# First norm of a two-layer hybrid backbone: modulation weights in four units of two feature tiles, k and the first q tile summed unit by unit

## The chip, the cores and the metric

The kernel runs on one core of one Trainium2 chip. A core has TensorE (matmuls into PSUM; the profile splits it into PE, the matmuls, and PEld, the weight loads), VectorE (DVE), ScalarE (ACT), GpSimd (POOL) and SyncE (SP, which here only issues DMAs). The metric is the device time of one execution in microseconds (us). Before the change it is 1147.22 us, the median of 3 runs (1147.14 to 1147.23).

## The reference, cut to what matters

Two layers work on 256 latent tokens (x) and 256 context tokens (ctx) of 1024 features. The part that the change touches is the very first step of layer 0: an RMS norm of both streams, its modulation by two vectors that are themselves matrix products, and the first columns of the input projection.

```python
m_lat = jnp.split((silu(c)     @ mod_w[0] + mod_b[0]), 6)      # shift, scale, gate, ...
m_ctx = jnp.split((silu(c_ctx) @ mod_w[0] + mod_b[0]), 6)
h_lat = rms_norm(x,   norm_g[0, 0]) * (1 + m_lat[1]) + m_lat[0]
h_ctx = rms_norm(ctx, norm_g[0, 0]) * (1 + m_ctx[1]) + m_ctx[0]
p  = h_lat @ even_w_in          # q, k, v of the attention, inputs of the HGRN2 heads
pc = h_ctx @ even_w_in
```

All of the rest (window attention, HGRN2, output projection, SwiGLU, then the retention layer with its own) follows from `p` and `pc`, and reaches the output through a long row of projections.

## The kernel before, in words

Features lie on the 128 partitions, so the 1024 features are 8 feature tiles, and a tile of `h` is 128 features by 512 tokens (256 latent, then 256 context). Every projection is done in three matmuls for each weight block of 128 by 128: the weight's rounded part times the rounded `h`, the same times the remainder of `h`, and the remainder of the weight times the rounded `h` (`mm3`, lines 336 to 338). The weights come as pieces of 8 blocks (512 KB, `load_raw`, line 258, three buffers); ACT makes the rounded part (`whi`, line 268), DVE the remainder (`wlo`, line 269), up to `LOOK` = 2 pieces ahead (`ensure`, four buffers).

The start of the kernel, in order of the program: `small`, 129 KB of constants, `x` in 8 DMAs of 128 KB, `ctx` in 4 of 256 KB, and then the modulation weights of shift and scale, 8.4 MB as 32 DMAs of 256 KB (line 130). They are four quarters of eight tiles: two for scale (chunk 1), two for shift (chunk 0), each 512 output features wide. The second half of these tiles borrows buffers of the weight pieces, of the later modulation weights (`mr`) and of `h`.

Inside a block with a manual schedule (lines 485 to 524) each engine keeps the order of the program: squares (ACT, line 445) and their sum over the feature tiles (DVE, line 449), one matmul with ones for each stream (line 453), Ln and Exp for the reciprocal root (lines 290 and 456); then for each quarter the product `mod0a` (16 matmul instructions, line 175, a copy to SBUF on ACT, line 178) and `mod0b` (4 small products that turn it onto the partitions, line 185, and `mod_finish` on DVE, lines 154 and 158). `scaled` (DVE, line 459) needs scale alone; `shifted` makes the rounded `h` (ACT, line 465) and the remainder (DVE, line 466) and needs shift, that is the last two quarters. Pieces 0 to 2 are converted among these.

Outside the manual block a planner fixes each engine's order: an instruction that is ready may be put into a gap of an engine ahead of earlier lines. The first such instructions are `p1`, the group with the columns of k and of the first q tile (line 891): all latent columns with the feature tile as the outer loop, then all context columns (2 tiles of columns, 8 feature tiles, 3 matmuls, twice, so 96 matmuls of 256 columns). Then `p2` (the other q tiles and v, 96 matmuls of 512 columns, pieces 2 to 5) and `tokgroup`. Each 1600 columns of such work call `tick`, which lets background work proceed: the later modulation vectors (`mod_one`, one task of 512 KB for each `MODE` = 2.3 ticks in this stage, two for a task that runs on TensorE) and the lanes of the attention.

Of the kernel before, what the change touches and what calls it, by code (L numbers as in the profile page):

```python
# [7 lines left out]
F32 = mybir.dt.float32  # L8
# [3 lines left out]
AF = mybir.ActivationFunctionType  # L12
ALU = mybir.AluOpType
# [19 lines left out]
N_PIECE = N_BLOCKS // PIECE  # L33
LOOK = 2
# [3 lines left out]
FA = 2  # L38
PES = [3]
ORD = [2, 3, 4, 5]  # L40
MODE = 2.3
TICK = 1600
ADEL = 5
HD1,HD2,HD3,HD4=[1, 1, 1, 2]
# [18 lines left out]
S_LB = S_OG + 1  # L63
# [5 lines left out]
def hybrid_kernel(ctx, tc, xT, wst, mw0, mwT, small, cbc, cst, imask, dmat, out, order):  # L69
    nc = tc.nc  # L70
# [34 lines left out]
    x = [cp.tile([P, L], F32, tag=f"x{k}", name=f"x{k}") for k in range(KD)]  # L105
    xc = [u((P, 2, L)) for _ in range(KD // 2)]
    for k in range(KD):
        nc.sync.dma_start(x[k][:], xT[:, k, LAT])
    for k in range(KD // 2):
        nc.sync.dma_start(xc[k][:], xT[:, 2 * k:2 * k + 2, CTX])  # L110

    def xs(k, s):
        return x[k][:] if s == 0 else xc[k // 2][:, k % 2, :]

    con0 = [u() for _ in range(3)]
    mws = []
    for i in range(32):
        if 16 <= i < 22:
            if i % 2 == 0:
                pair = rawp.tile([P, 2, NT], F32, tag="raw", name=nm("raw"))  # L120
            t = pair[:, i % 2, :]
        elif 22 <= i < 28:
            if i % 2 == 0:
                pair = mp.tile([P, D], F32, tag="mr", name=nm("mr"))
            t = pair[:, (i % 2) * NT:(i % 2 + 1) * NT]
        elif i < 16:
            t = u()[:]
        else:
            t = hp.tile([P, NT], F32, tag="h", name=nm("mw"))[:]
        nc.sync.dma_start(t, mw0[i // 8, i % 8])  # L130
        mws.append(t)
# [123 lines left out]
    def load_raw(r):  # L255
        if r not in raws:
            t = rawp.tile([P, RAW, P], F32, tag="raw", name=nm("raw"))
            nc.sync.dma_start(t[:].rearrange("p b n -> p (b n)"), wst[r])
            raws[r] = t

    def ensure(p):
        for q in range(len(pieces), min(p + LOOK, N_PIECE - 1) + 1):
            r = q
            load_raw(r)
            src = raws.pop(r)
# [153 lines left out]
    class Norm:  # L419
# [6 lines left out]
        def pre(self, k):  # L426

            hi, lo = u(dt=F32R), u(dt=F32R)
            sh = mvec(self.l, self.s, 3 * self.j, k).to_broadcast([P, 2])
            split(sh, hi[:, L:LW], lo[:, L:LW])  # L430
            g = gsv[:, self.l, self.j, self.s, k:k + 1]
            A.activation(hi[:, LAT], x[k][:], AF.Copy, scale=g)
            V.scalar_tensor_tensor(lo[:, LAT], x[k][:], g, hi[:, LAT].bitcast(F32), ALU.mult, ALU.subtract)
# [47 lines left out]
    def upd(l, ch, s, m, ps):  # L481
        sl = LAT if s == 0 else CTX
        V.scalar_tensor_tensor(xs(m, s), ps[:, sl], mvec(l, s, ch, m), xs(m, s), ALU.mult, ALU.add)  # L483

    manual[0] = True
    with tc.manual_schedule():
        h = new_h()
        ns = [Norm(0, 0, s, h) for s in range(2)]
        for n in ns:
            for k in range(KD):  # L490
                n.add(k)
            n.stats()
        for r in range(3):
            load_raw(r)
        ts_ = [u() for _ in range(KD)]

        def scaled(s, ks):
            for k in ks:
                ns[s].scaled(k, ts_[k][:, ns[s].sl])

        mod0a(0)
        mod0a(1)
        mod0b(0)
        scaled(0, range(4))
        mod0a(2)
        mod0b(1)
        scaled(0, range(4, 8))
        scaled(1, range(4))
        mod0a(3)
        mod0b(2)  # L510
        scaled(1, range(4, 8))
        mod0b(3)
# [5 lines left out]
        for n in ns:
            for k in range(KD):
                if n.s == 0 and k in (1, 4):  # L520
                    ensure(k // 4 - LOOK)
                n.shifted(k, ts_[k][:, n.sl])
        ensure(0)
# [9 lines left out]
    omh = cp.tile([P, 4], F32, tag="omh", name="omh")
    nomh = cp.tile([P, 4], F32, tag="nomh", name="nomh")
    lbh = cp.tile([P, 4], F32, tag="lbh", name="lbh")
    l0, l1 = sml[:, S_LB:S_LB + 4], sml[:, S_LB + 4:S_LB + 8]
    mx, e0, e1 = sm(4), sm(4), sm(4)
    V.tensor_tensor(mx, l0, l1, ALU.max)
    V.tensor_tensor(e0, l0, mx, ALU.subtract)
    V.tensor_tensor(e1, l1, mx, ALU.subtract)  # L540
    A.activation(e0, e0, AF.Exp)
    A.activation(e1, e1, AF.Exp)
    V.tensor_tensor(e1, e0, e1, ALU.add)
    V.reciprocal(e1, e1)
    V.tensor_tensor(e0, e0, e1, ALU.mult)
    V.tensor_scalar(omh[:], e0, -0.5, 0.5, ALU.mult, ALU.add)
    V.tensor_scalar(nomh[:], e0, 0.5, -0.5, ALU.mult, ALU.add)
    V.tensor_scalar(lbh[:], e0, 0.5, 0.5, ALU.mult, ALU.add)
# [770 lines left out]
```

## Time and profile before

| | |
|---|---|
| median of 3 runs | 1147.22 us |
| the profiled execution | 1146.45 us, of which the span of the trace 1144.6 us |
| PE busy | 1116.4 us (98%) |
| PEld busy | 996.9 us (87%) |
| DVE busy | 767.4 us (67%) |
| ACT busy | 554.0 us (48%) |
| HBM read | 177.56 MB, 156 GB/s over the span |

The page gives each engine's busy time and its share of the span, and the chain of work that ended last. Idle time of an engine that is not the bottleneck costs nothing. A timeline row gives start, duration, engine, line, operation, output and inputs, the count of merged instructions, and in brackets the idle time before them with what ended it. An engine's name with a q is its queue: SPq rows are issues of DMAs and not the transfers. A matmul's duration includes its pipeline, so the rate of a series is read from the distance of the starts.

### The profile page before, as it was taken

The numbers are of one execution on the slowest core, as the hardware profiler recorded it, in microseconds if no ns is written. First come the engines' busy times: TensorE is split into PE (matmuls) and PEld (weight loads), VectorE is DVE, ScalarE is ACT, GpSimd is POOL, SyncE is SP. The second block draws the span as 40 slices with busy tenths as digits, with TensorE's granted clock in tenths as the row PEclk, the third lists the DMA queues.
The fourth block names the chain that finished last, engine by engine and source line by source line (L and its number), as shares of the span: only waits on it lengthen the run. The fifth ranks groups of instructions, "written<-read, shape, count | busy, mean of one in ns | idle before, by whom it ended". The sixth has DMA issues, their size and how long they took to land.

```text
span 1144.6 us, 18866 instructions
## 1 busy us (share of the span) xinstructions
PE 1116.4 (98%) x7514; PEld 996.9 (87%) x7514; DVE 767.4 (67%) x1399; ACT 554.0 (48%) x948; POOL 20.8 (2%) x46
## 2 busy tenths in 40 slices
PE   3999999999999999999999998999999999999998
PEld 1777877888998888988888898999999999999998
DVE  3877698899798557357883678374646577555553
ACT  5676676664753231123322476454445657544441
POOL 0012000000000000000000000000000000000000
PEclk9999999999999999999999999999999999999999
DMA  9987221326237446247983324343434265655553
GB/s 329 349 235 184 92 65 66 112 74 202 94 113 241 143 147 202 77 139 237 324 308 109 95 75 129 111 131 109 148 94 147 92 203 167 192 183 181 184 183 109
DMA packets 56121, 182.46 MB, mean 159 GB/s; under 512 B 6368, under 2 KB 9824, under 8 KB 55904
## 3 DMA queue, kind: packets, MB, share of 16 engines
q1 hardware_dynamic: 53648, 176.45, 47.6%
q0 software_dynamic: 2240, 4.72, 1.7%
q8 instruction: 59, 0.97, 0.4%
q14 instruction: 30, 0.25, 0.1%
q10 hardware_dynamic: 144, 0.08, 0.0%
HBM read 177.56 MB, written 1.05 MB: 156 GB/s over the span
## 4 chain that ended last, share of the span: by engine, by line
PE 84%; DVE 10%; ACT 3%; DMA 1%; issue 1%; DVEq 0%; ACTq 0%; SPq 0%
PE mm L338 23%; PE mm L337 23%; PE mm L336 23%; PE ax L337 2%; PE ax L336 2%; PE ax L338 2%; DVE wlo L269 2%; DMA raw<-in_wst_dram 1%; PE ax L175 1%; PE ax L656 1%; ACT whi L268 1%; PE ax L675 1%; DVE u L459 1%; PE mm L411 1%; PE mm L409 1%
## 5 line engine op out<-in xcount | busy, mean ns | idle before, releaser
L268 ACT ACTIVATE whi<-raw 128x1024 fp32r<-128x1024 f32 x230 | 243.3, 1059 | 403.0 <-PE mm L337 242.9
L269 DVE TENSOR_TENSOR wlo<-raw,whi 128x1024 fp32r<-128x1024 f32 x230 | 280.7, 1222 | 166.5 <-ACT whi L268 165.9
L336 PE MATMUL mm<-hh,whi 128*128 128x256 f32 (+1 forms) x1072 | 362.2, 339 | 1.2 <-ACT whi L268 0.9
L338 PE MATMUL mm<-hh,wlo 128*128 128x256 f32 (+1 forms) x1072 | 361.6, 338 | 0.6 <-DVE wlo L269 0.6
L337 PE MATMUL mm<-hl,whi 128*128 128x256 f32 (+1 forms) x1072 | 362.0, 338 | 0.1
L337 PE MATMUL mm<-u,whi 128*128 128x256 f32 (+2 forms) x768 | 236.9, 309 | 0.0
L338 PE MATMUL mm<-u,wlo 128*128 128x256 f32 (+2 forms) x768 | 236.7, 308 | 0.0
L336 PE MATMUL mm<-u,whi 128*128 128x256 f32 (+2 forms) x768 | 236.3, 308 | 0.3 <-DVE x L483 0.3
L338 PEld LDWEIGHTS mm<-hh,wlo 128*128 128x128 f32 x1072 | 204.4, 191 | 21.8 <-DVE wlo L269 0.8
L336 PEld LDWEIGHTS mm<-hh,whi 128*128 128x128 f32 x1072 | 204.2, 191 | 21.9 <-ACT whi L268 0.9
L337 PEld LDWEIGHTS mm<-hl,whi 128*128 128x128 f32 x1072 | 204.3, 191 | 20.2 <-DVE hl L466 0.3
L336 PEld LDWEIGHTS mm<-u,whi 128*128 128x128 f32 x768 | 146.4, 191 | 7.9 <-issue 0.4
L338 PEld LDWEIGHTS mm<-u,wlo 128*128 128x128 f32 x768 | 146.6, 191 | 7.2
L337 PEld LDWEIGHTS mm<-u,whi 128*128 128x128 f32 x768 | 146.6, 191 | 7.1
L233 DVE CUSTOM_DVE_ANT_0 mr<-mr,cb 128x1024 f32<-128x1024 f32 x72 | 87.1, 1222 | 13.2 <-DMA mr<-in_mwT_dram 12.6
L416 ACT ACTIVATE u<-u 128x512 fp32r<-128x512 f32 (+1 forms) x84 | 43.0, 526 | 36.7 <-DVE u L1007 17.3
L1007 DVE TENSOR_TENSOR u<-u,mm 128x512 f32<-128x512 f32 (+1 forms) x40 | 22.1, 553 | 44.7 <-PE mm L338 44.7
L233 DVE CUSTOM_DVE_ANT_0 u<-mr,cb 128x1024 bf16<-128x1024 f32 x40 | 48.4, 1219 | 2.8 <-DMA mr<-in_mwT_dram 1.5
L417 DVE TENSOR_TENSOR u<-u,u 128x512 fp32r<-128x512 f32 (+1 forms) x84 | 46.5, 565 | 5.0 <-ACT u L416 4.9
L336 PE MATMUL ax<-u,u 128*128 128x256 f32 x160 | 45.9, 287 | 3.1 <-ACT u L416 3.1
L483 DVE SCALAR_TENSOR_TENSOR x<-mm,modv,x 128x256 f32<-128x256 f32 x48 | 22.4, 480 | 36.1 <-PE mm L338 36.1
L337 PE MATMUL ax<-u,u 128*128 128x256 f32 x160 | 46.0, 287 | 0.0
(220 smaller groups left out, 1216.4 us busy)
## 6 DMA issues: line engine op xcount, KB each, us to landing
raw<-in_wst_dram SPq DMA_DIRECT2D x230, 512.0 KB, 3.8
mr<-in_mwT_dram SPq DMA_DIRECT2D x80, 512.0 KB, 4.5
u<-in_mw_dram SPq DMA_DIRECT2D x16, 256.0 KB, 5.2
u<-u POOLq DMA_DIRECT2D x20, 128.0 KB, 5.7
u<-in_dmat_dram POOLq DMA_DIRECT2D x8, 256.0 KB, 3.0
raw<-in_mw_dram SPq DMA_DIRECT2D x6, 256.0 KB, 5.2
mr<-in_mw_dram SPq DMA_DIRECT2D x6, 256.0 KB, 5.2
x<-in_xT_dram SPq DMA_DIRECT2D x8, 128.0 KB, 3.4
```

The costliest lines, as they stand in the source:

```text
L175: T.matmul(ps[32 * g:32 * g + 32, :], cT[:, k, :], mws[nt * 8 + k], start=(k < 4), stop=(k >= 4), skip_group_check=True)
L233: V.tensor_tensor_reduce(o, mr[:], cb[:, s, :], 1.0, 0.0, ALU.mult, ALU.add, mvec(l, s, ch, k))
L268: A.activation(hi[:], src[:], AF.Copy)
L269: V.tensor_tensor(lo[:], src[:], hi[:].bitcast(F32), ALU.subtract)
L336: T.matmul(o, w[0], a[0], start=first, stop=False, skip_group_check=shared)
L337: T.matmul(o, w[0], a[1], start=False, stop=False, skip_group_check=shared)
L338: anchor[0] = T.matmul(o, w[1], a[0], start=False, stop=last, skip_group_check=shared)
L409: T.matmul(ps[t][:], a[0], w[0], start=(k == 0), stop=False)
L416: A.activation(hi, src, AF.Copy)
L417: V.tensor_tensor(lo, src, hi.bitcast(F32), ALU.subtract)
L483: V.scalar_tensor_tensor(xs(m, s), ps[:, sl], mvec(l, s, ch, m), xs(m, s), ALU.mult, ALU.add)
L1007: V.tensor_tensor(g[:, 0:w], g[:, 0:w], ps[2 * i + 1][:, 0:w], ALU.mult)
```

## The change

The modulation weights of shift and scale are laid out in four units. Unit p holds scale and shift of feature tiles 2p and 2p+1 (256 columns of each), so one `mod0a`/`mod0b` gives all that these two tiles of `h` need. `x` is loaded in two DMAs of 512 KB with 4 KB in a row on a partition (before: 1 KB), `ctx` in four with 2 KB in a row. The order of the DMAs is: unit 0, x, ctx, weight piece 0, units 1 and 2, piece 1, and after the first feed unit 3, piece 2 and the constants. The sum of squares over feature tiles is taken on TensorE (16 products with ones in float32, no sums on DVE), squares are of two feature tiles each, Ln and Exp use one table set, loaded once with the constants of the HGRN2 gates. `mod0a` leaves its result in PSUM, and `mod0b` makes the copy.

`p1` is written into the manual block: `dense(k)` does all 512 tokens of feature tile k for both column tiles (6 matmuls of 512 columns), between the products of the units. Only pieces 0 and 1 are converted in the block (`look[0]` is 0 in it and `LOOK` after). `p1` calls no `tick`; `MODE` is 1.9 for 2.3.

```diff
-MODE = 2.3
+MODE = 1.9
...
-        parts[nt] = u()
-        A.activation(parts[nt][:], ps[:], AF.Copy)
-
-    def mod0b(nt):
-        ch, half = 1 - nt // 2, nt % 2
-        part = parts[nt]
+        parts[p] = ps
+
+    def mod0b(p):
+        part = u()
+        A.activation(part[:], parts[p][:], AF.Copy)
...
+        for i, ch in enumerate((1, 0)):
+            mod_finish(0, ch, 2 * p, 2 * p + 2, ps2[:, 2 * i:2 * i + 2, :].rearrange("p c s -> p s c"))
...
+        load_raw(0)
+        mw_load(1)
+        mw_load(2)
+        load_raw(1)
+        lb_consts()
+        mod0a(0)
+        mod0b(0)
+        stat = []
         for n in ns:
+            ps = axb()[:, 0:L]
+            for j in range(4):
+                q = u((P, 2, L))
+                src = xl[j // 2][:, 2 * (j % 2):2 * (j % 2) + 2, :] if n.s == 0 else xc[j][:]
+                if n.s and j % 2:
+                    V.tensor_tensor(q[:], src, src, ALU.mult)
+                else:
+                    A.activation(q[:], src, AF.Square)
+                for i in range(2):
+                    T.matmul(ps, ones, q[:, i, :], start=(j + i == 0), stop=(j + i == 4))
+            stat.append(ps)
+        for n, ps in zip(ns, stat):
+            n.r = u()[:, 0:L]
+            A.activation(n.r, ps, AF.Ln, bias=epst[:], scale=1.0 / D)
+            A.activation(n.r, n.r, AF.Exp, scale=-0.5)
...
+        def dense(k, js):
+            for j in js:
+                w = take('ein', k, j)
+                o = p1[j][:]
+                T.matmul(o, w[0], HS[k][0], start=(k == 0), stop=False)
+                T.matmul(o, w[0], HS[k][1], start=False, stop=False)
+                anchor[0] = T.matmul(o, w[1], HS[k][0], start=False, stop=(k == KD - 1))
+
+        def feed(p):
+            for k in (2 * p, 2 * p + 1):
+                t = scaled(k)
+                if k % 4 == 0:
+                    ensure(k // 4)
+                shifted(k, t)
+
         mod0a(1)
+        feed(0)
+        mw_load(3)
+        load_raw(2)
...
+        dense(0, J)
+        mod0b(1)
+        feed(1)
+        dense(1, J)
+        mod0a(2)
+        dense(2, J)
+        mod0b(2)
+        feed(2)
+        dense(3, J)
+        mod0a(3)
+        dense(4, J)
+        mod0b(3)
+        feed(3)
+        for k in range(5, KD):
+            dense(k, J)
         A.activation(cb[:], cb[:], AF.Silu)
...
-    p1 = group('ein', [E_AK, E_AQ], K8, HS, sls=(LAT, CTX))
```

## Rows read from the trace of the kernel before

**Rows 1.** The page: the busy line of the engines (us, share of the span, instructions), and the chain that ended last, by engine.

```profile
PE 1116.4 (98%) x7514; PEld 996.9 (87%) x7514; DVE 767.4 (67%) x1399; ACT 554.0 (48%) x948; POOL 20.8 (2%) x46
...
PE 84%; DVE 10%; ACT 3%; DMA 1%; issue 1%; DVEq 0%; ACTq 0%; SPq 0%
```

**Rows 2.** Busy time by stretch: the stretch and its length, busy us of PE, PEld, DVE, ACT, POOL (with counts), the granted clock of TensorE as a share of full, the busy share of the DMA engines, GB/s.

```profile
0.00:50.82 50.82, 31.39 (x197) 20.57 (x197) 28.00 (x73) 32.03 (x57) 1.25 (x6) 0.97 0.94 348
50.82:95.00 44.18, 44.18 (x189) 34.52 (x188) 36.36 (x64) 28.71 (x37) 5.32 (x11) 1.00 0.74 215
```

**Rows 3.** Timeline of PE from the statistics to the first sum of `p1`.

```profile
19.10 1.22 PE L453 MATMUL ax<-u,con 128*128 128x256 f32 x2 [6.54 <-DVE u L449]
20.25 5.73 PE L175 MATMUL ax<-u,cT 128*32 128x512 f32 x32
25.91 1.05 PE L185 MATMUL ax<-con,u 128*128 128x2 f32 x8
...
33.73 1.95 PE L185 MATMUL ax<-con,u 128*128 128x2 f32 x16
36.53 0.50 PE L336 MATMUL mm<-hh,whi 128*128 128x256 f32 x2 [0.85 <-ACT whi L268]
```

**Rows 4.** Timeline of PEld in the products of the quarters: four loads at the lower and at the upper rate, and the wait for the last tile of the modulation weights.

```profile
23.67 0.20 PEld L175 LDWEIGHTS ax<-u,cT 128*32 128x32 f32 x4 [0.66 <-issue]
24.52 0.12 PEld L175 LDWEIGHTS ax<-u,cT 128*32 128x32 f32 x4 [0.65 <-DMA raw<-in_mw_dram]
24.95 0.12 PEld L175 LDWEIGHTS ax<-u,cT 128*32 128x32 f32 x4 [0.31 <-issue]
...
32.75 0.14 PEld L175 LDWEIGHTS ax<-mw,cT 128*32 128x32 f32 x2 [0.51 <-DMA mw<-in_mw_dram]
```

**Rows 5.** Timeline of PE: two sums of `p1` at the lower rate, the last of `p1`, and the first two of `p2`.

```profile
40.73 0.41 PE L336 MATMUL mm<-hh,whi 128*128 128x256 f32 x1
40.95 0.41 PE L337 MATMUL mm<-hl,whi 128*128 128x256 f32 x1
...
50.70 0.28 PE L338 MATMUL mm<-hh,wlo 128*128 128x256 f32 x1
50.82 0.40 PE L336 MATMUL mm<-hh,whi 128*128 128x512 f32 x1
51.05 0.40 PE L337 MATMUL mm<-hl,whi 128*128 128x512 f32 x1
```

**Rows 6.** Busy time by stretch, columns as in rows 2, around the start of `p1`.

```profile
35.00:36.00 1.00, 0.67 (x7) 0.59 (x6) 1.00 (x3) 0.98 (x2) 0.00 (x0) 1.00 1.01 404
...
37.00:38.00 1.00, 0.53 (x3) 0.30 (x2) 1.00 (x2) 1.00 (x3) 0.00 (x0) 1.00 1.03 382
38.00:39.00 1.00, 0.78 (x3) 0.78 (x4) 1.00 (x4) 1.00 (x3) 0.00 (x0) 0.58 1.13 443
39.00:40.00 1.00, 1.00 (x7) 1.00 (x6) 1.00 (x2) 1.00 (x4) 0.00 (x0) 0.50 1.01 425
...
41.50:42.00 0.50, 0.50 (x6) 0.50 (x5) 0.50 (x3) 0.50 (x2) 0.00 (x0) 0.93 1.00 410
```

**Rows 7.** Timeline of ACT and DVE together, in order of time: the copy of a late line, the statistics' last Exp, the copy of a quarter's result, `mod_finish`, `scaled`, the conversions, `shifted`, and the Silu of `cb`.

```profile
6.74 0.29 ACT L1042 ACTIVATE idr<-con 128x128 fp32r<-128x128 f32 x1
...
20.85 1.28 ACT L456 ACT_TABLE_LOAD   x1
...
22.15 0.42 ACT L456 ACTIVATE u<-u 128x256 f32<-128x256 f32 x1
...
27.00 0.17 DVE L154 TENSOR_TENSOR modv<-ax,sml 128x8 f32<-128x8 f32 x1 [7.96 <-PE ax L185]
...
27.40 1.67 DVE L459 SCALAR_TENSOR_TENSOR u<-x,gsv,u 128x256 f32<-128x256 f32 x4
...
33.83 0.60 ACT L178 ACTIVATE u<-ax 128x512 f32<-128x512 f32 x1 [4.27 <-PE ax L175]
...
37.58 1.04 ACT L268 ACTIVATE whi<-raw 128x1024 fp32r<-128x1024 f32 x1
...
39.27 1.22 DVE L269 TENSOR_TENSOR wlo<-raw,whi 128x1024 fp32r<-128x1024 f32 x1
...
40.41 4.83 DVE L466 SCALAR_TENSOR_TENSOR hl<-u,modv,hh 128x256 fp32r<-128x256 f32 x12
...
44.38 1.28 ACT L524 ACT_TABLE_LOAD   x1
...
45.67 1.91 ACT L524 ACTIVATE cb<-cb 128x2048 f32<-128x2048 f32 x1
...
47.49 1.04 ACT L268 ACTIVATE whi<-raw 128x1024 fp32r<-128x1024 f32 x1
```

**Rows 8.** Timeline of ACT late in the trace: Ln and Exp after one load of a table set that holds both.

```profile
739.80 1.28 ACT L292 ACT_TABLE_LOAD   x1
742.38 0.47 ACT L294 ACTIVATE u<-ax,eps 128x256 f32<-128x256 f32 x1 [1.29 <-PE ax L1153]
742.88 0.42 ACT L1156 ACTIVATE u<-u 128x256 f32<-128x256 f32 x1
```

**Rows 9.** Busy time by stretch, columns as in rows 2: the DMA rate while x and ctx come, and while the modulation weights come.

```profile
5.00:8.00 3.00, 0.00 (x0) 0.00 (x0) 1.03 (x7) 2.97 (x9) 0.00 (x0) 1.00 0.80 248
...
14.00:17.00 3.00, 0.00 (x0) 0.00 (x0) 1.27 (x3) 2.99 (x10) 0.00 (x0) 1.00 1.05 406
```

More of the change, by code (lines that the diff above doesn't have):

```diff
@@ L104, in hybrid_kernel, with xs, mw_load @@
     nc.sync.dma_start(con[:, 0:C_RCOS], cst[:, 0:C_RCOS])
-    x = [cp.tile([P, L], F32, tag=f"x{k}", name=f"x{k}") for k in range(KD)]
+    xl = [cp.tile([P, 4, L], F32, tag=f"x{j}", name=f"x{j}") for j in range(2)]
+    x = [xl[k // 4][:, k % 4, :] for k in range(KD)]
     xc = [u((P, 2, L)) for _ in range(KD // 2)]
-    for k in range(KD):
-        nc.sync.dma_start(x[k][:], xT[:, k, LAT])
-    for k in range(KD // 2):
[L110 to L131, printed above, removed]
+    def xs(k, s):
+        return x[k] if s == 0 else xc[k // 2][:, k % 2, :]
+    con0 = [u() for _ in range(3)]
+    mws = [None] * 4
+    def mw_load(p):
+        mws[p] = []
+        for i in range(KD):
+            if p < 3 or i >= 6:
+                t = u()[:]
+            else:
+                if i % 2 == 0:
+                    pair = mp.tile([P, D], F32, tag="mr", name=nm("mr"))
+                t = pair[:, i % 2 * NT:i % 2 * NT + NT]
+            nc.sync.dma_start(t, mw0[p, i])
+            mws[p].append(t)
+    mw_load(0)
+    for j in range(2):
+        nc.sync.dma_start(xl[j][:], xT[:, 0, 4 * j:4 * j + 4, :])
+    for k in range(KD // 2):
+        nc.sync.dma_start(xc[k][:], xT[:, 1, 2 * k:2 * k + 2, :])
     msk = cp.tile([P, 2, P], I32, tag="msk", name="msk")
@@ L169, in hybrid_kernel, with mod0a @@
     parts = {}
-    def mod0a(nt):
+    def mod0a(p):
         ps = axb()
@@ L174, in mod0a @@
             g = k % 4
-            T.matmul(ps[32 * g:32 * g + 32, :], cT[:, k, :], mws[nt * 8 + k], start=(k < 4), stop=(k >= 4),
+            T.matmul(ps[32 * g:32 * g + 32, :], cT[:, k, :], mws[p][k], start=(k < 4), stop=(k >= 4),
                      skip_group_check=True)
-        parts[nt] = u()
-        A.activation(parts[nt][:], ps[:], AF.Copy)
-    def mod0b(nt):
-        ch, half = 1 - nt // 2, nt % 2
-        part = parts[nt]
+        parts[p] = ps
+    def mod0b(p):
+        part = u()
+        A.activation(part[:], parts[p][:], AF.Copy)
         ps2 = axb((P, 4, 2))
@@ L185, in mod0b @@
             T.matmul(ps2[:, c, :], part[:, c * P:(c + 1) * P], sel, start=True, stop=True)
-        mod_finish(0, ch, half * 4, half * 4 + 4, ps2[:].rearrange("p c s -> p s c"))
+        for i, ch in enumerate((1, 0)):
+            mod_finish(0, ch, 2 * p, 2 * p + 2, ps2[:, 2 * i:2 * i + 2, :].rearrange("p c s -> p s c"))
     mod_tasks = [(0, c, k) for c in ORD for k in range(KD)] + [(1, c, k) for c in range(6) for k in range(KD)]
@@ L259, in load_raw @@
             raws[r] = t
+    look = [0]
     def ensure(p):
[L262 to L265, printed above, removed]
+        for q in range(len(pieces), min(p + look[0], N_PIECE - 1) + 1):
+            load_raw(q)
+            src = raws.pop(q)
             hi = wp.tile([P, PIECE, P], F32R, tag="whi", name=nm("whi"))
@@ L431, in pre @@
             g = gsv[:, self.l, self.j, self.s, k:k + 1]
[L432 to L433 removed]
+            A.activation(hi[:, LAT], x[k], AF.Copy, scale=g)
+            V.scalar_tensor_tensor(lo[:, LAT], x[k], g, hi[:, LAT].bitcast(F32), ALU.mult, ALU.subtract)
             self.p.append((hi[:, 0:LW], lo[:, 0:LW]))
@@ L483, in upd, with lb_consts @@
         V.scalar_tensor_tensor(xs(m, s), ps[:, sl], mvec(l, s, ch, m), xs(m, s), ALU.mult, ALU.add)
+    omh = cp.tile([P, 4], F32, tag="omh", name="omh")
+    nomh = cp.tile([P, 4], F32, tag="nomh", name="nomh")
+    lbh = cp.tile([P, 4], F32, tag="lbh", name="lbh")
+    def lb_consts():
+        l0, l1 = sml[:, S_LB:S_LB + 4], sml[:, S_LB + 4:S_LB + 8]
+        mx, e0, e1 = sm(4), sm(4), sm(4)
+        V.tensor_tensor(mx, l0, l1, ALU.max)
+        V.tensor_tensor(e0, l0, mx, ALU.subtract)
+        V.tensor_tensor(e1, l1, mx, ALU.subtract)
+        A.preload_act_table_set("natural_log_exp_and_others")
+        A.activation(e0, e0, AF.Exp)
+        A.activation(e1, e1, AF.Exp)
+        V.tensor_tensor(e1, e0, e1, ALU.add)
+        V.reciprocal(e1, e1)
+        V.tensor_tensor(e0, e0, e1, ALU.mult)
+        V.tensor_scalar(omh[:], e0, -0.5, 0.5, ALU.mult, ALU.add)
+        V.tensor_scalar(nomh[:], e0, 0.5, -0.5, ALU.mult, ALU.add)
+        V.tensor_scalar(lbh[:], e0, 0.5, 0.5, ALU.mult, ALU.add)
     manual[0] = True
@@ L488, in hybrid_kernel @@
         ns = [Norm(0, 0, s, h) for s in range(2)]
-        for n in ns:
[L490 to L501, printed above, removed]
-        mod0a(1)
[L503 to L512, printed above, removed]
+        load_raw(0)
[6 more added lines that the diff above has]
+        stat = []
+        for n in ns:
+            ps = axb()[:, 0:L]
[4 more added lines that the diff above has]
+                    V.tensor_tensor(q[:], src, src, ALU.mult)
+                else:
+                    A.activation(q[:], src, AF.Square)
+                for i in range(2):
+                    T.matmul(ps, ones, q[:, i, :], start=(j + i == 0), stop=(j + i == 4))
+            stat.append(ps)
@@ new lines, in hybrid_kernel, with scaled, shifted @@
+        for n, ps in zip(ns, stat):
+            n.r = u()[:, 0:L]
+            A.activation(n.r, ps, AF.Ln, bias=epst[:], scale=1.0 / D)
+            A.activation(n.r, n.r, AF.Exp, scale=-0.5)
+        HS = [(a[:], b[:]) for a, b in h]
+        p1 = [mmb() for _ in range(2)]
+        def scaled(k):
+            t = u()
+            for n in ns:
+                n.scaled(k, t[:, n.sl])
+            return t
+        def shifted(k, t):
+            for n in ns:
+                n.shifted(k, t[:, n.sl])
@@ L518, in hybrid_kernel @@
[L518 to L523, printed above, removed]
+        J = range(2)
+        dense(0, J)
[13 more added lines that the diff above has]
+            dense(k, J)
@@ L524, in hybrid_kernel @@
         A.activation(cb[:], cb[:], AF.Silu)
+    look[0] = LOOK
     manual[0] = False
-    HS = [(a[:], b[:]) for a, b in h]
     K8 = list(range(8))
     E_AK, E_AQ, E_AV, E_I, E_H, E_G = 0, 1, 5, 6, 10, 22
[L533 to L548, printed above, removed]
     nsk = cp.tile([P, 8], F32, tag="nsk", name="nsk")
@@ L1189, in hybrid_kernel @@
     for m in range(KD):
-        nc.sync.dma_start(out[m * P:(m + 1) * P, :], x[m][:])
+        nc.sync.dma_start(out[m * P:(m + 1) * P, :], x[m])
     assert len(order) == N_BLOCKS and mod_pos[0] == len(mod_tasks)
@@ L1266 @@
     cbc = np.stack([I['c'][0], I['c_ctx']])
-    m0 = mw[0][:, :2048].reshape(8, P, 4, 512)
-    mw0 = np.stack([m0[:, :, n] for n in (2, 3, 0, 1)])
+    m0 = mw[0][:, :2048].reshape(8, P, 2, 4, 256)
+    mw0 = np.stack([np.concatenate([m0[:, :, 1, p], m0[:, :, 0, p]], axis=2) for p in range(4)])
     mt = np.concatenate([mw[0].T[2048:], mw[1].T], axis=0).reshape(80, P, D)
```

6 lines of the change are left out of this document (3 added, 3 removed).

## The prediction

> **What bounds the kernel now.** I read the page first: PE is busy for 98% of the span and holds 84% of the chain that ended last [rows 1], so an edit elsewhere counts only where TensorE waits. The busy time by stretch says where that is: in the first 50.8 us PE is busy for 31.4 us, and from there to 95 us for all of it [rows 2]. The place to look at is the head. Its timeline shows small products of the modulation weights and the first real sum at 36.53 us, and `p2` at 50.82 us, with sums every 0.23 us and no stall behind it [rows 3, 5]. What follows 50.82 us is full, and keeps its order. So the change is worth what the start of `p2` moves, as long as its weights are ready.
>
> Three clocks run in the head. The DMA queue moves about 250 GB/s while x and ctx come in short rows and 406 GB/s later [rows 9]; the last tile of the modulation weights lands at 32.75 us [rows 4]. TensorE runs at its lower level (1.2 GHz) at first, by its own distances: four loads of L175 every 0.85 us until 24.5 us, every 0.43 us from there [rows 4]; and once more from 38 to 41.5 us, granted 0.50 to 0.58, after a stretch with PE busy about half of each microsecond [rows 6]. The third is the chain of norm, modulation and split on ACT and DVE.
>
> **The change part by part.** I follow the new order by hand to the start of `p2`, with durations of this execution.
>
> *DMAs.* Before the last unit's last tile now come 11.75 MB instead of 10.7: pieces 0 and 1 (0.52 MB each) go ahead of it. At 406 GB/s that is 2.6 us later; x and ctx (2.1 MB) at 406 in place of 250 GB/s give back up to 3.2 us [rows 9]. So unit 3 lands between 32.1 and 35.4 us; I take 32.7, as now, because the long rows of x are nearest to those of the modulation weights. By the same rate unit 0 is there at 9.2 us, x at 11.8, ctx at 14.4, unit 1 at 21, unit 2 at 26, piece 2 at 34. None of the SP issues moved waits for a computed result except two buffers of unit 3, long free. The MB of `cb` lands at about 38 us, before it is needed. All DMA of the old head still moves, so nothing is saved there.
>
> *Statistics.* Removed: 14 sums on DVE and table loads of 1.28 us (as at 20.85 us, rows 7). That Ln and Exp of one set need no load between them is seen late in the trace, where Exp follows at once [rows 8]; if two came all the same on the path of the second stream, they would cost 2.6 us, otherwise nothing. Added: 14 more float32 products with ones. Each is two passes of 256 columns; four column groups of 512 take 0.85 us at the lower level and 0.43 at the upper [rows 4], so one pass of 256 is half of that and a product again 0.85 or 0.43 us. They queue on PE behind unit 0. Unit 0: last tile 9.2, result copied on ACT 1.1 us later (as 32.75 to 33.83 us, rows 4 and 7), copy 0.60, products L185 1.05 [rows 3]: PE is free at 12.1 us. From a start at 19.10 us the level rose at 24.5 us [rows 3, 4]; the same 5.2 us from 12.1 give six products at 0.85, and ten at 0.43: 21.6 us. All at the upper level would end at 19.0, all at the lower at 25.8; the squares are ready by about 16 us and don't bound it. With 0.4 us of latency, Ln 0.47 and Exp 0.42 [rows 8] the second root is ready at 22.9 us. Before, it was ready at 22.6 [rows 7]: the statistics gain nothing. The gain has to come from the sums that now run in between.
>
> *Feeds.* After the root DVE needs for each feature tile two `scaled` and two remainders, 0.40 to 0.42 us each [rows 7], and ACT two rounded tiles beside it: 1.7 us with one wait, 3.4 us for a unit. Feed 0 also has piece 0: `whi` 1.05 after the root, `wlo` 1.15; its last remainder is done 4.7 us after the root, at 27.6. Then the unit's round trip: ACT's copy stands behind the rounded tiles, which end 0.4 us before the last remainder; 0.6 for the copy, 0.1, then 1.1 from the first L185 to `mod_finish` (25.91 to 27.00, rows 3 and 7): DVE waits 1.4 us; `mod_finish` now has three operations at 0.2. So a further feed takes 1.4 + 0.6 + 3.4 = 5.4 us: feed 1 is done at 33.0, feed 2 with piece 1 at 39.5, feed 3 at 44.9. Behind the waiting `mod_finish` stands all of DVE, behind the waiting copy all of ACT. The last sum has one matmul ahead of the last remainder and five behind it, 0.23 us each [rows 5]: `p2` could start at 46.1.
>
> *Does TensorE keep up?* At the upper level `dense(k)` is 1.4 us and `mod0a` 1.7 us [rows 5, 4]; unit 2's product ends at 31.8 and unit 3's at about 37, each after its DMA and before ACT can take the copy. So in this case PE hides behind DVE, where before 96 sums of 256 columns stood bare from 36.5 to 50.8 us.
>
> *What I add.* (a) Between 23.3 us (end of unit 1's product) and 28.7 us PE has only one `dense` and L185 to do. A similar thin stretch was followed by the lower level until 41.5 us [rows 6]. If that happens, `dense(1)` and part of unit 2's product cost 1.6 us more, with nothing to hide them; I take 1.0 (bounds 0 and 1.6 for one fall). (b) Piece 2 isn't converted in the manual block any more. The planner does fill gaps with later lines: the copy at L1042 sits at 6.74 us [rows 7]. So I expect `whi` and `wlo` of piece 2, ready from 34 us, in gaps of the feeds; where the gap is smaller than the 1.05 and 1.22 us, the feed is pushed. Between 0 and 2.3 us, I take 1.0 (DVE's wait for the last unit, 1.4 us, is the nearest gap and fits one).
>
> *Ticks.* Before, `p1`, `p2` and `tokgroup` made 40,960 columns, 25 ticks of 1600; now 32,768, 20 ticks. At 2.3 and 1.9 ticks for a task both end with ten tasks done (eight single, one double: 8 x 2.3 + 4.6 = 23.0 of 25; 8 x 1.9 + 3.8 = 19.0 of 20). The next double task comes one tick later. In the old run the tasks of `p1` couldn't start on DVE before `cb`'s Silu ended at about 47.5 us [rows 7], so DVE's load behind the start of `p2` is about the same. Cost nothing, bounds minus and plus 0.5 us, since the stretch to 95 us has no idle PE [rows 2].
>
> **Sum.** 46.1 + 1.0 + 1.0 = 48.1 us in place of 50.82: 2.7 us less. Against the execution's 1146.45 us (span 1144.6 and 1.85 around it) that is 1143.7; its time stands 0.77 below the median, and the same saving from the median gives 1144.5 us. A measurement here can tell about 0.2% (2.3 us) from no change, so the forecast lies just outside it.
>
> **Rivals.**
>
> *A: piece 2 behind `cb`'s Silu.* If the planner leaves it in order, ACT ends the rounded tiles at 45.4, loads the table and does the Silu in 3.1 us (44.38 to 47.49, rows 7), `whi` at 48.5 to 49.55, `wlo` to 50.75. The third matmul of `p2` waits for it, so `p2` starts as if at 50.3: saving 0.5, 1146.7 us. For it: line order, and in the old trace this Silu did stand ahead of a conversion [rows 7]. Against: L1042 again, and that the old piece hadn't a free place earlier. The Trainium skill ("ScalarE: Activation LUTs", What ACT_TABLE_LOAD costs) adds a drain to each switch and puts it at 2.66 us; the trace shows 1.29 us from load to Silu, so here the measurement decides; by the page this rival would be at 1148.1.
>
> *B: slower, TensorE's level.* PE now waits between its sums from 23 to 46 us. If the lower level returns and stays, `dense` takes 2.56 us (six of 0.427) and `mod0a` 3.4: from 26.0 us eight sums, two products and three L185 are 20.5 + 6.8 + 3.2 = 30.5 us, PE is the bound, `p2` starts at 56.4, 1152.8 us. It decides from about half of that work at the lower level, where the 17.6 us of work at the upper reach past 50.8. For it: rows 6. Against: the level came back in the old run 3.4 us after PE was full. The Trainium skill ("TensorE: Matmul & The Clock Gate", HAM oscillation — how this bites in real kernels) describes this: tiles summed one by one with waits between them, and the clock lost at each. No row of this trace shows it repeated; by that rule it would be this case.
>
> *C: the extras don't come.* Piece 2 fits its gaps, no fall of the level, and the statistics run at the upper level because unit 0's products have raised it: 46.1 - 2.6 = 43.5, saving 7.3, 1139.9 us. Unit 3's landing doesn't forbid it: 32.7 us and a product, round trip, feed and sum (1.1 + 1.75 + 0.6 + 3.4 + 1.2) end at 40.8. The full amount needs three things at once.
>
> *D: the order of later stages isn't kept,* and a wait comes up behind `p2`. The old trace has no slack there on PE [rows 2]; nothing in the diff touches these lines, and the amount is open in both directions.
>
> **Chances.** Forecast 0.50 (its own range 1142.3 to 1146.8, from the bounds of (a) and (b)); A 0.20; B 0.12; C 0.13; D 0.05. Below 1144.9: a little over half of the forecast, all of C, and part of D: 0.45. Within 0.2%: the rest of the forecast, most of A: 0.39. Above 1149.5: B, and little of A and D: 0.16. The range of 1140.8 to 1149.0 leaves out B and half of C.
>
> **What would show it.** First real sum (`dense(0)`) near 24 us in place of 36.5; root of the second stream near 23; last remainder of feed 3 near 46 to 47; first 512-column sum of `p2` near 48 with `whi` of piece 2 done earlier; granted clock low once, at about 29 to 32 us. Wrong if `p2`'s first sums wait for ACT L268 or the conversion stands behind the Silu (A), if the granted clock is 0.50 through most of 26 to 46 us (B), or if PE shows new waits behind `p2` (D).

## The result and the profile after

The changed kernel takes 1157.79 us (median; 1156.96 to 1159.77), the kernel before, run beside it, 1147.22 us. The ratio is 1.0095, 95% interval 1.0083 to 1.0107: slower by 10.6 us, where 2.7 us less was predicted, and outside the forecast's range of 1140.8 to 1149.0 us. The profiled execution took 1158.14 us (span 1156.4).

The page of the changed kernel: busy line, chain that ended last, and two groups of sums with the idle time before them.

```profile
PE 1127.9 (98%) x7494; PEld 1000.7 (87%) x7494; DVE 764.2 (66%) x1393; ACT 553.5 (48%) x939; POOL 20.6 (2%) x46
...
PE 76%; DVE 11%; DMA 6%; ACT 5%; issue 2%; SPq 0%; DVEq 0%; ACTq 0%
...
L338 PE MATMUL mm<-hh,whi 128*128 128x512 f32 (+1 forms) x1040 | 353.9, 340 | 3.7 <-ACT whi L270 3.4
...
L338 PE MATMUL mm<-u,whi 128*128 128x256 f32 (+2 forms) x768 | 236.9, 310 | 5.2 <-DVE u L1052 3.1
```

PE's share of the chain is 76% where it was 84% [rows 1]: time went to ACT and DMA. PE is busy 11.5 us longer with 20 instructions fewer; part of that is the lower clock in the stretches below. The two groups name one wait for a conversion (3.4 us) and one for a DVE result (3.1 us).

Busy time by stretch, columns as in rows 2.

```profile
0.00:50.82 50.82, 38.42 (x173) 23.18 (x174) 22.90 (x63) 27.98 (x45) 1.25 (x6) 0.93 0.95 359
50.82:95.00 44.18, 42.77 (x181) 32.87 (x180) 33.45 (x57) 31.72 (x40) 4.24 (x8) 1.00 0.63 177
...
35.00:40.00 5.00, 4.45 (x27) 1.93 (x25) 4.28 (x7) 1.86 (x3) 0.00 (x0) 1.00 1.03 417
40.00:45.00 5.00, 1.38 (x5) 1.06 (x6) 0.88 (x2) 3.07 (x5) 0.00 (x0) 0.88 1.03 420
45.00:50.00 5.00, 5.00 (x15) 4.13 (x16) 3.97 (x9) 1.23 (x3) 0.00 (x0) 0.50 0.61 215
```

The head was to be fuller; instead PE stands almost still from 40 to 45 us and runs at its lower level (0.50) for the next 5. The timeline of ACT says why:

```profile
15.35 1.28 ACT L533 ACT_TABLE_LOAD   x1
...
17.13 1.28 ACT L534 ACT_TABLE_LOAD   x1
...
18.86 1.28 ACT L533 ACT_TABLE_LOAD   x1
...
20.64 1.28 ACT L534 ACT_TABLE_LOAD   x1
21.94 0.42 ACT L534 ACTIVATE u<-u 128x256 f32<-128x256 f32 x1
...
35.13 1.06 ACT L270 ACTIVATE whi<-raw 128x1024 fp32r<-128x1024 f32 x1 [1.70 <-DMA raw<-in_wst_dram]
...
41.74 1.06 ACT L270 ACTIVATE whi<-raw 128x1024 fp32r<-128x1024 f32 x1 [4.75 <-DMA raw<-in_wst_dram]
...
43.50 0.57 ACT L182 ACTIVATE u<-ax 128x512 f32<-128x512 f32 x1
```

ACT loads a table four times around Ln and Exp. Until 35.13 and 41.74 it waits for weight pieces 2 and 3, still on their way: the planner put their conversions among the feeds. The copy of unit 3 (L182), whose product was done at 37.4 us, stands behind them and starts at 43.50. PE stands too. The planner moved up two matmuls of `p2` (the second at 39.05), and the next one waits for piece 3:

```profile
39.05 0.40 PE L339 MATMUL mm<-hl,whi 128*128 128x512 f32 x1
42.85 0.50 PE L338 MATMUL mm<-hh,whi 128*128 128x512 f32 x1 [3.40 <-ACT whi L270]
44.13 1.87 PE L185 MATMUL ax<-con,u 128*128 128x2 f32 x8 [0.78 <-ACT u L182]
```

The head is the smallest part. I compared the start of each matmul that both kernels have, group by group, and took the median difference (after less before): it is 0.8 us at 70 to 75 us, 2.5 from 76 to 100, 6.3 at 420 to 600, 11.3 from 610 on and 11.7 at the end. So most of the loss comes behind the edited lines.

The first step, 1.7 us near 76 us, stands at the start of the token group: PE waits for ACT's copy of a bank of `p2`, which is queued behind a weight conversion that itself waits 3.86 us for PE. ACT and PE of the changed kernel:

```profile
76.04 1.06 ACT L270 ACTIVATE whi<-raw 128x1024 fp32r<-128x1024 f32 x1 [3.86 <-PE mm L339]
77.00 0.58 ACT L604 ACTIVATE u<-mm 128x512 f32<-128x512 f32 x1
...
77.64 0.50 PE L411 MATMUL mm<-whi,hh 128*128 128x512 f32 x1 [1.41 <-ACT u L604]
```

In the kernel before the same copy stands one conversion earlier, and PE goes on without a wait:

```profile
70.80 0.58 ACT L558 ACTIVATE u<-mm 128x512 f32<-128x512 f32 x1
```

Further on, two stretches show new waits of PE; here is the later one, DVE, PE and ACT of the changed kernel in order of time:

```profile
616.43 1.23 DVE L234 CUSTOM_DVE_ANT_0 mr<-mr,cb 128x1024 f32<-128x1024 f32 x1 [1.01 <-DMA mr<-in_mwT_dram]
...
617.74 1.23 DVE L234 CUSTOM_DVE_ANT_0 mr<-mr,cb 128x1024 f32<-128x1024 f32 x1
...
619.10 0.68 DVE L1052 TENSOR_TENSOR u<-u,mm 128x512 f32<-128x512 f32 x1
...
619.82 0.63 ACT L418 ACTIVATE u<-u 128x512 fp32r<-128x512 f32 x1 [4.17 <-DVE u L1052]
...
619.84 0.50 PE L338 MATMUL mm<-u,whi 128*128 128x512 f32 x1 [3.08 <-DVE u L1052]
...
621.03 0.63 PE L339 MATMUL mm<-u,whi 128*128 128x512 f32 x1
621.46 0.63 PE L340 MATMUL mm<-u,wlo 128*128 128x512 f32 x1
```

L234 is the multiply and sum of a background task (the modulation of later stages), on 512 KB that a DMA brings. L1052 is a gate of the feed-forward stage, a product on DVE that reads a PSUM bank; this one is the 20th of 40 and the last ahead of the stage's output sums (`mm<-u`). Its own input was done on PE at 614.7 us, but it is queued behind the last task. PE stands for 3.08 us and starts 0.06 us after the gate's end, while ACT's split of the gate's result (L418) still runs. So, by the program, PE waits for the bank that the gate reads and not for the result: the pool has four banks, and the first group of output sums takes four. From 620.6 us on PE runs its sums every 0.43 us in place of 0.23 until 624.0.

In the kernel before the same run of tasks ends 18 us earlier, ahead of the 19th gate (600.96). The 20th has no task ahead of it: DVE is idle for 3.37 us and starts it as soon as PE's sums are done, and PE doesn't wait:

```profile
599.60 1.23 DVE L233 CUSTOM_DVE_ANT_0 mr<-mr,cb 128x1024 f32<-128x1024 f32 x1
...
600.96 0.68 DVE L1007 TENSOR_TENSOR u<-u,mm 128x512 f32<-128x512 f32 x1
...
608.56 0.69 DVE L1007 TENSOR_TENSOR u<-u,mm 128x512 f32<-128x512 f32 x1 [3.37 <-PE mm L338]
```

The earlier stretch goes through the tasks' loads. SP issues the transfer of a weight piece at 273.92 us, behind three loads of tasks (before: 267.87). ACT's conversion waits 6.56 us for it (before: 4.71), with nothing but copies and a table load between it and the split L418 that PE waits for. L926 on DVE, which makes the input of that split and stands behind the last task, had ended 1.15 us before the split began:

```profile
273.92 0.33 SPq L259 DMA_DIRECT2D raw<-in_wst_dram  x1
...
278.16 1.06 ACT L270 ACTIVATE whi<-raw 128x1024 fp32r<-128x1024 f32 x1 [6.56 <-DMA raw<-in_wst_dram]
...
279.50 0.74 DVE L926 SCALAR_TENSOR_TENSOR u<-ax,ogq,u 128x512 f32<-128x512 f32 x1
...
281.39 0.61 ACT L418 ACTIVATE u<-u 128x512 fp32r<-128x512 f32 x1
...
282.05 1.21 PE L338 MATMUL mm<-u,whi 128*128 128x512 f32 x4 [1.58 <-ACT u L418]
```

The same transfer and conversion in the kernel before:

```profile
267.87 0.33 SPq L258 DMA_DIRECT2D raw<-in_wst_dram  x1
...
272.33 1.06 ACT L268 ACTIVATE whi<-raw 128x1024 fp32r<-128x1024 f32 x1 [4.71 <-DMA raw<-in_wst_dram]
```

A third step, 1.5 us between 185 and 215 us, was not followed up.

What moved the tasks? Counted through both programs, behind `tokgroup` the counter `tickn` stands at 2.0 before and at 1.0 after (and 960 against 768 columns toward the next tick). Since `p1` calls no `tick` now and `MODE` is 1.9, nearly every later task falls one tick later. That is the theory to test (T): a head that loses some 2.5 us, and a counter that loses the rest. Rival: the reordered head itself shifts the planner's order.

### The profile page after: what moved, and what is told of

It reads as the page before. It is cut to its first block, busy times and chain, and to the rows that moved or that the text cites. A ratio compares the mean times of both kernels' runs of the same rounds, so it can differ in the third digit from the quotient of the medians.

```text
span 1156.4 us, 18794 instructions
## 1 busy us (share of the span) xinstructions
PE 1127.9 (98%) x7494; PEld 1000.7 (87%) x7494; DVE 764.2 (66%) x1393; ACT 553.5 (48%) x939; POOL 20.6 (2%) x46
## 4 chain that ended last, share of the span: by engine, by line
PE 76%; DVE 11%; DMA 6%; ACT 5%; issue 2%; SPq 0%; DVEq 0%; ACTq 0%
PE mm L338 21%; PE mm L339 21%; PE mm L340 20%; DMA mr<-in_mwT_dram 4%; PE ax L339 2%; PE ax L338 2%; PE ax L340 2%; DVE wlo L271 2%; DMA raw<-in_wst_dram 1%; DVE mr L234 1%; ACT whi L270 1%; DVE u L764 1%; PE mm L411 1%; PE ax L702 1%; PE mm L412 1%
## 5 line engine op out<-in xcount | busy, mean ns | idle before, releaser
L338 PE MATMUL mm<-hh,whi 128*128 128x512 f32 (+1 forms) x1040 | 353.9, 340 | 3.7 <-ACT whi L270 3.4
L339 PE MATMUL mm<-hl,whi 128*128 128x512 f32 (+1 forms) x1040 | 352.9, 339 | 0.0
L340 PE MATMUL mm<-hh,wlo 128*128 128x512 f32 (+1 forms) x1040 | 352.4, 339 | 0.0
L338 PEld LDWEIGHTS mm<-hh,whi 128*128 128x128 f32 x1040 | 197.9, 190 | 26.2 <-ACT whi L270 3.8
L340 PEld LDWEIGHTS mm<-hh,wlo 128*128 128x128 f32 x1040 | 197.9, 190 | 20.9 <-issue 0.2
L339 PEld LDWEIGHTS mm<-hl,whi 128*128 128x128 f32 x1040 | 197.9, 190 | 20.1 <-issue 0.2
L234 DVE CUSTOM_DVE_ANT_0 mr<-mr,cb 128x1024 f32<-128x1024 f32 x72 | 87.1, 1221 | 14.1 <-DMA mr<-in_mwT_dram 13.5
L418 ACT ACTIVATE u<-u 128x512 fp32r<-128x512 f32 (+1 forms) x84 | 42.9, 526 | 41.0 <-DVE u L1052 23.8
L1052 DVE TENSOR_TENSOR u<-u,mm 128x512 f32<-128x512 f32 (+1 forms) x40 | 22.1, 552 | 44.4 <-PE mm L340 44.4
L234 DVE CUSTOM_DVE_ANT_0 u<-mr,cb 128x1024 bf16<-128x1024 f32 x40 | 48.3, 1218 | 0.8 <-DMA mr<-in_mwT_dram 0.7
```

The costliest lines, as they stand in the source:

```text
L234: V.tensor_tensor_reduce(o, mr[:], cb[:, s, :], 1.0, 0.0, ALU.mult, ALU.add, mvec(l, s, ch, k))
L338: T.matmul(o, w[0], a[0], start=first, stop=False, skip_group_check=shared)
L339: T.matmul(o, w[0], a[1], start=False, stop=False, skip_group_check=shared)
L340: anchor[0] = T.matmul(o, w[1], a[0], start=False, stop=last, skip_group_check=shared)
L418: A.activation(hi, src, AF.Copy)
L1052: V.tensor_tensor(g[:, 0:w], g[:, 0:w], ps[2 * i + 1][:, 0:w], ALU.mult)
```

## Experiments

All of e1 to e8 compute the same outputs. Ratios are to the kernel before, run beside them (medians 1146.84 to 1147.27 us).

**e1: the kernel before, ticks late.** No line of the head is touched.

```diff
     modt[0] = MODT[0]
+    tickn[0] -= 1
+    cnt[0] -= 192
```

> The kernel before, with the tick count set back by one tick (and 192 columns) after the token group, so that the background tasks stand where the changed kernel has them; its head is untouched. Theory T (the loss behind 200 us, some 9 of the 10.6 us, comes from the background tasks falling one tick later): 1151 to 1156 us, with a wait of TensorE of about 3 us for L1007 near 605 to 615 us. Rival R (the loss there follows from the changed head, through the planner's order, and not from the tick): within 1 us of 1147.2.

Measured 1157.82 us, ratio 1.0092 (1.0077 to 1.0107): the whole loss, without the change. The differences to the kernel before are 0.7 us at 50 to 100, 2.0 at 200, 4.4 at 350 to 600, 10.9 from 610. The waits of PE are the same two; the later one in e1:

```profile
616.77 1.23 DVE L233 CUSTOM_DVE_ANT_0 mr<-mr,cb 128x1024 f32<-128x1024 f32 x1 [0.25 <-DMA mr<-in_mwT_dram]
...
618.13 0.68 DVE L1009 TENSOR_TENSOR u<-u,mm 128x512 f32<-128x512 f32 x1
...
618.87 0.79 PE L336 MATMUL mm<-u,whi 128*128 128x512 f32 x1 [3.98 <-DVE u L1009]
```

This is the 20th gate again, behind the last task. So the tick alone is enough, and it costs more than I gave it.

**e2: the changed kernel, ticks put back.** `tickn[0] += 1` and `cnt[0] += 192` at the same place.

> The changed kernel with the tick count set forward by one tick (and 192 columns) after the token group, as the kernel before has it. Theory T: the loss behind 200 us goes, 1148 to 1151 us (the head's loss of about 2.5 us at 80 us stays). Rival R: 1156 to 1159 us as the changed kernel.

Measured 1149.23 us, ratio 1.0017 (1.0007 to 1.0026). The difference is 0.9 us at 70 to 75 us, 2.6 behind the start of the token group, and stays between 2.6 and 3.0 to the end; no wait near 610. The tick was 1157.79 - 1149.23 = 8.6 us of the loss; the other 2 are the head and the wait at the token group. The parts don't add up exactly (10.7 alone in e1). The wait at the gate is 3.08 us in the changed kernel and 3.98 in e1: a head that is already late changes how far the gate stands behind the tasks.

**e3: the changed kernel, conversions held back.** Pieces 2 to 4 are converted where the block says, behind the last feed.

```diff
         feed(3)
+        ensure(4)
```

> The changed kernel with weight pieces 2 to 4 converted inside the manual block behind the last feed, so that the planner can't put their conversions between the feeds. Theory H (in the head ACT stood still 4.8 us for the transfer of piece 3, with the last unit's copy and feed behind it): no wait of TensorE for ACT near 40 us, second group of q tiles starting at 46 to 48 us, the work at 80 us 3 to 4 us earlier than in the kernel before (changed kernel: 2.5 later); the total 5 to 6 us below the changed kernel, 1151 to 1153, if the later stages lose the same. Rival (the last unit is late for another reason, its landing or TensorE's lower clock): head and total as in the changed kernel.

Measured 1156.79 us, ratio 1.0083 (1.0065 to 1.0101). It is 2.2 us ahead of the kernel before at 70 to 75 us, so the head is mended, but only 0.4 to 0.9 ahead from 76 to 150, where I had given 3 to 4; then 3.5 us behind at 400 and 9.6 from 610, with PE waiting 4.15 us for the gate at 618.16. The total is 1.0 us below the changed kernel's and not 5 to 6. A good head doesn't cure the ticks.

**e4: both edits.**

> Both edits: pieces 2 to 4 converted behind the last feed, and the tick count set forward by one tick. Theories T and H together: 1142.5 to 1145 us, below both kernels. If R holds in place of T: 1148 to 1153 us.

Measured 1145.28 us, ratio 0.9983 (0.9969 to 0.9996), 0.3 us above the range I gave. The feeds end without a wait for a transfer, and `p2` starts where I had put it (48.1):

```profile
46.11 2.94 ACT L270 ACTIVATE whi<-raw 128x1024 fp32r<-128x1024 f32 x3
...
48.06 0.39 PE L338 MATMUL mm<-hh,whi 128*128 128x512 f32 x1
```

But of 2.8 us gained there only 0.5 is left at 100 us. PE waits 1.41 us at 74.60 for ACT's copy of a bank of `p2`, which stands behind a conversion that itself waits 4.38 us for PE. All six kernels with the new head (the changed one, e2, e3, e4, e6 and e7) have this wait, 1.41 us each, and lose 1.7 us there; the kernel before, e1, e5 and e8 don't have it. So it comes with the new head, and neither the ticks nor the held conversions change it. Why the planner queues the copies there was not tried.

**e5: e1, but from task 31 on at the old ticks.** The lines stand in `mod_one`.

```diff
         i = mod_pos[0]
+        if i == 30:
+            tickn[0] += 1
+            cnt[0] += 192
```

> The kernel before, with the background tasks one tick late from the end of the token group on, as in e1, but put back to the old ticks from task 31 of the list on (task 30 is the last late one). Theory (each late task costs where it stands, and the largest part of the loss is the burst that comes late near 610 us): the shift against the kernel before is as in e1 up to some 300 us (0.7 at 100, 2 at 230, about 4 at 300), nothing is added at 610, the wait of PE there for VectorE's divisions is gone, time 1150 to 1152. Rival (once the order of the stages has shifted, the loss at 610 comes from that and not from the late tick): 1156 to 1158 with the wait of 3 to 4 us at 605 to 615 still there.

(What the expectations call divisions are the tasks' multiply-and-sum instructions.) Measured 1151.16 us, ratio 1.0034 (1.0021 to 1.0048). The difference steps from 1.5 to 4.7 us near 280, is 5.1 us from 350 to 650, and nothing is added at 610: the last task stands ahead of the 19th gate again, and the 20th, at 613.68, waits for PE alone. The wait at 280 is still there:

```profile
280.15 1.66 PE L339 MATMUL mm<-u,whi 128*128 128x512 f32 x4 [2.12 <-ACT u L419]
...
607.78 1.23 DVE L236 CUSTOM_DVE_ANT_0 mr<-mr,cb 128x1024 f32<-128x1024 f32 x1 [0.52 <-DMA mr<-in_mwT_dram]
...
609.14 0.68 DVE L1012 TENSOR_TENSOR u<-u,mm 128x512 f32<-128x512 f32 x1
...
613.68 0.69 DVE L1012 TENSOR_TENSOR u<-u,mm 128x512 f32<-128x512 f32 x1 [0.97 <-PE mm L341]
```

The late ticks cost at separate places: up to task 30 the stretch from 185 to 290 us, from task 31 on the gate at 610. The rival falls.

**e6: e4 with the table loaded ahead of the roots.**

```diff
+        A.preload_act_table_set("natural_log_exp_and_others")
         for n, ps in zip(ns, stat):
```

> e4 with one more load of the table that holds both Ln and Exp, put into the head's written order behind the squares and ahead of the two roots, so that neither Ln nor Exp loads one in between. Theory: two to three of ACT's four loads of 1.28 us go from the chain of the roots, the last Exp ends 1.3 to 2.6 us sooner than 22.36, p2 starts 1 to 2 us sooner than e4's 48.06, and half of it or more is kept: 1143.5 to 1144.8. Rival (what the head gains is given back at the token group, where ACT's copies of p2's banks stand behind a conversion that waits for PE): p2 starts sooner but the wait there grows from 1.41 us by as much, 1145 to 1146.

Measured 1142.56 us (1142.12 to 1144.57), ratio 0.9965 (0.9951 to 0.9978): faster than both kernels, and a little better than the theory's range. ACT and PE of e6:

```profile
15.37 1.28 ACT L531 ACT_TABLE_LOAD   x1
16.94 0.48 ACT L534 ACTIVATE u<-ax,eps 128x256 f32<-128x256 f32 x1 [0.29 <-PE ax L529]
17.45 0.42 ACT L535 ACTIVATE u<-u 128x256 f32<-128x256 f32 x1
20.39 0.47 ACT L534 ACTIVATE u<-ax,eps 128x256 f32<-128x256 f32 x1 [2.53 <-PE ax L529]
20.90 0.42 ACT L535 ACTIVATE u<-u 128x256 f32<-128x256 f32 x1
...
44.68 0.39 PE L338 MATMUL mm<-hh,whi 128*128 128x512 f32 x1
...
71.32 0.50 PE L411 MATMUL mm<-whi,hh 128*128 128x512 f32 x1 [1.41 <-ACT u L606]
```

Three of four loads are gone and the second root is ready at 21.32 us, 1.04 sooner than in the changed kernel (21.94 + 0.42), a little less than the 1.3 to 2.6 that I gave. The clock stays at 1.00 in every stretch of the head, which it didn't in e4, so part of the 3.4 us that `p2` starts sooner than in e4 (1 to 2 given) is probably that. Of 6.1 us against the kernel before, 5.5 are left at 75 us, 3.8 behind the start of the token group and 4.0 at the end: the wait at the token group is the same 1.41 us and didn't grow, so the rival falls too.

**e7: `MODE = 1.8` in place of 1.9, and the table load; conversions not held.** By the count this gives `tickn` 20 - 10 x 1.8 = 2.0 again; the columns toward the next tick stay at 768, as in the changed kernel.

> The changed kernel with two edits: the first period's length of a tick count is 1.8 in place of 1.9, which gives the later stages the counter that the kernel before has there, and the load of the table as in e6; pieces 2 to 4 are converted where the planner puts them, not held. Theory (the ticks are the whole of the late loss, and the head's loss is the conversions that wait for transfers): no step near 290 or 610 us, p2 starts 49 to 52, a wait of ACT for a transfer of 3 to 5 us in 35 to 45, time 1147.5 to 1149.3 as e2's 1149.23 less what the loads cost. Rival (the constant moves the early tasks and with them the order in 50 to 110 us so that the loss comes back): 1153 or more.

Measured 1150.33 us, ratio 1.0030 (1.0019 to 1.0041), 1.0 us above the theory's range: no gap at 610, so one constant of the change holds most of the loss, and the 192 columns aren't needed for it. ACT still waits 3.09 and 4.77 us for pieces 2 and 3, until 34.76 and 41.38. Behind the start of the token group e7 is 1.6 us behind the kernel before where e2 is 2.6, so its head is 1.0 us better. But that is lost again in small steps from 280 us on, to 3.8 us at the end, which the theory missed; where from was not tried.

**e8: the kernel before, ticks early.** As e1 with `+=`.

> The kernel before with the background tasks one tick early from the end of the token group on: the mirror of e1. Theory (a late task is what costs, since the bursts of divisions on VectorE then end behind the moment at which PE wants the operand queued after them; an early one does no harm): both bursts end sooner, no wait of PE near 280 or 610, time 1145.5 to 1148, within 0.2% of before. Rival (any shift of the background tasks against the planner's order costs, early or late): 1150 or more, with a new wait of PE somewhere.

Measured 1148.14 us, ratio 1.0006 (0.9997 to 1.0016): no change that can be told, and no wait above 0.3 us at 280 or 610. But the bursts don't end sooner, as the theory has it: the last tasks start at 272.70 and 601.94 us, before at 272.44 and 599.60, and the tasks stand between the same gates as before. So e8 shows that this shift leaves the order alone, and doesn't test what tasks that really come a gate sooner would do. Its profiled execution is 0.15 us behind from 300 to 650 us and 2.75 us behind at the end; the runs spread from 1145.91 to 1151.26.

## Why the prediction was wrong

**The step that failed is *Ticks*.** It said that both kernels "end with ten tasks done", that "the next double task comes one tick later", and "Cost nothing, bounds minus and plus 0.5 us, since the stretch to 95 us has no idle PE". The counting was right; the price was read at the wrong place. The remainder of the counter isn't used up by the next task, it goes on, and the price lies where a task on DVE, or its load on SP, stands ahead of something PE wants: 610 and 280 us. e1 gives it as 10.7 us alone, e2 as 8.6 in the changed kernel. The rows that would have warned stand in the trace of before, 600 us in: the last tasks stand right ahead of the 19th gate (600.96). DVE has room behind it, but tasks that come one gate later stand ahead of the 20th, and there PE has only the output sums left, which need its bank. I looked only as far as `p2`, because "what follows 50.82 us is full, and keeps its order". Full it was; but that nothing waits now doesn't say by how much.

**What the start of `p2` moves** isn't what the change is worth, even with the ticks put back: e4 starts `p2` 2.8 us sooner and e6 6.1, and both lose 1.7 us at the token group, where the prediction had a full PE and an order that is kept.

**Rival D** ("the order of later stages isn't kept") is what happened, at a chance of 0.05 and with "the amount is open in both directions". The diff leaves the lines in order, as I said; the phase of the tasks between them moved, and the planner with it.

**What I add (b)** was mis-sized: 1.0 us, bounds 0 to 2.3, for piece 2 in gaps of the feeds. I had the planner filling gaps, and it did; I took for granted that it fills them with what has landed. It took pieces 2, 3 and 4, and ACT waited 1.70 + 4.75 us for two of them. With the pieces held (e4), `p2` starts at 48.06, and the work at 70 to 75 us comes 3.2 us sooner than in e2. So with the ticks alone put back the changed kernel still isn't faster: e2 is 2.1 us above the kernel before.

**What I add (a)**, one fall of the clock, is right in kind: e4 has one (granted 0.89 at 25 to 30 us and 0.77 at 30 to 35), e6 none. In the changed kernel it comes later and lasts longer (45 to 50 us at 0.50), behind a stretch in which PE, waiting for ACT, was busy for 1.38 of 5 us. Rival B, a level that stays low through the head, isn't seen. Rival C comes nearest in e6: no fall of the level, nothing of piece 2 among the feeds, `p2` at 44.68 us (43.5 given), and 4.3 us saved of the 7.3 given.

**Statistics**: the second root was forecast for 22.9 and came at 22.4, by two errors that nearly cancel. The products ran from 12.6 to 19.8 us, not to 21.6, since PE was at its upper level from their start; and the loads between Ln and Exp, which I costed at 2.6 us and then left out, were there: the planner put the load of the common table ahead of `cT`'s Silu, whose own load replaced it. e6 shows 1.04 us for three of them.

**DMAs and Feeds** held until the planner's conversions came: unit 3 was there for its product at 35.45 us (landing forecast at 32.7, 35.4 at the latest), the first sum came at 24.15 (near 24), and the last remainders of feeds 0 and 1 ended at 27.2 and 32.5 (27.6 and 33.0).

**The Sum** was right for the head alone: had the ticks been kept and the pieces held, 1144.5 was forecast and e4 gave 1145.28. But even this agrees partly by chance. e4's gain at `p2` (2.8 us) is mostly lost at the token group, a wait I hadn't looked for; its median lies 1.9 us below the kernel before (0.5 to 3.6 by the interval), its profiled execution, 1145.67, 0.8 us below that of before.

What stays open: one tick is some 1600 columns, or about 2.2 us at three matmuls of 0.23 us for 512, yet one pair of tasks came at 530.38 and 531.64 us where it had been at 513.23 and 514.49, 17 us later, when PE was 6.3 us late. The gates are 10.9 us apart there, and the pair starts 2.59 us behind the 11th gate in the one kernel (510.64) and 2.59 us behind the 12th in the other (527.79): it fell back by one whole gate. The same holds of the last five tasks, in the changed kernel, e1 and e3 alike; in the other runs they stand ahead of the 19th gate. Why the planner turns one tick into a whole gate was not tried.

## What to carry to other kernels

A counter that paces background work carries its remainder past the edit; compare its state at the end of the edited part, and if it differs, set it back (one constant or one line) before judging the edit. A full engine behind the edit doesn't show slack: look for the places where background work, or its loads, stands just ahead of a result, a bank or a transfer that the full engine needs. Where a planner fills gaps, an operation whose input is still in flight blocks everything queued behind it: pin the order of conversions and table loads where it matters.

## What the runs showed of the hardware that was not expected

A wait of 3.08 us of PE in a full stretch of the changed kernel cost 5 us: sums that followed 0.8 us later ran every 0.43 us until 624.0. In the profiled execution of e5 the granted clock read 0.95 in nearly every stretch, yet its sums of 512 columns start every 0.23 us, as in e6 at 1.00, and its time of 1151.89 us is at most 1.5 us above the other three runs of e5, whose clock read 0.996 or 0.997. Busy time by stretch of both, columns as in rows 2, first e5:

```profile
300.00:600.00 300.00, 299.96 (x1515) 256.37 (x1514) 205.54 (x327) 98.43 (x135) 0.00 (x0) 0.95 0.55 182
```

and e6:

```profile
300.00:600.00 300.00, 300.00 (x1487) 255.44 (x1486) 207.52 (x327) 94.11 (x123) 0.00 (x0) 1.00 0.58 188
```

So here a granted clock that read a few per cent low was no sign of lost time; the spacing of the matmuls would have shown it.
